# Where the weight sums of the second FFN product are formed, and when its residuals are added

## The chip, the cores and the metric

The kernel runs on one core of a Trainium2 chip. The metric is the time of one execution on the device, in microseconds (us). TensorE (PE in the profile) multiplies matrices, with the loads of its stationary operand shown apart (PEld). VectorE (DVE), ScalarE (ACT) and GpSimd (POOL) do elementwise work. SyncE (SP) issues every transfer between HBM and the on-chip memory (DMA); sixteen DMA engines carry them.

## The reference, cut to what matters

One encoder layer for 17 blocks of 128 tokens: a mixer, a layer norm, a feed-forward network (FFN), and another layer norm. Change and prediction concern the FFN.

```python
D_MODEL = 1024; D_FF = 4 * D_MODEL; ALPHA = 2 ** 0.25
def squared_relu_ffn(x, w1, w2):
    h = jnp.square(jax.nn.relu(jnp.einsum('bld,df->blf', x, w1)))
    return jnp.einsum('blf,fd->bld', h, w2)
...
xp = layer_norm(ALPHA * xp + hp, ln1_g[l], ln1_b[l])                                    # x1 in the kernel
xp = layer_norm(ALPHA * xp + squared_relu_ffn(xp, w_ff1[l], w_ff2[l]), ln2_g[l], ln2_b[l])
```

## The kernel before

The program is one stream: the mixer, the projection `out_proj`, then `ffn`. The order of instructions on each engine is not written by hand. A scheduler takes the program and lets an instruction go out ahead of earlier ones when its operands and its buffer are free by its own timing; the result is a fixed queue for each engine, and an engine works through its queue in order. A buffer of a pool is used again only when its last reader is done, and the transfer that fills it then waits in SP's queue with all that stands behind it.

**Numbers.** Every fp32 operand of the FFN is split into a high and a low part (`split`: a cast on ACT, then a subtraction on DVE), and each product is three matmuls (high·high, high·low, low·high: `PASSES`).

**Seven products for eight.** Both FFN products work on 2x2 blocks and replace eight block products by seven (the scheme of Strassen and Winograd), at the price of sums of blocks on both sides. The products are numbered 1 to 7. `Sums` forms the sums and keeps them in HBM: `x_piece` those of the tokens (`xv`), `w1_piece` those of `w_ff1` (`w1s`), `w2_piece` those of `w_ff2` (`w2s`).

**First product** (matmul line L880). The tokens go in three batches b = 0, 1, 2 (384, 384 and 320 columns, `TOKENS`); in each, 16 steps g over `w_ff1`. A step runs its seven products in the order 1, 6, 2, 7, 5, 4, 3 with 12 matmuls each. A step needs the seven weight blocks of its g (`load_w1`: tiles `w1l`, `w1r`, `w1s`, 1.75 MB), and a batch needs seven token tiles (`load_x`: stage `xr`, two buffers, then `xt`, which are freed by the last step of the batch before). `hc` and `hs` leave as the sums `hv`. In batches 1 and 2 every second step also calls `w2_piece` for one g: it loads the four blocks b11, b12, b21, b22 of `w_ff2` in two transfers of 512 KB (`w2p`), makes T1 = b12 - b11, b22 - b12, T2 = b22 - T1 and T2 - b21 in four subtractions (L792 to L795), and stores them in two transfers of 512 KB (`w2s`). The tiles come from the pool `stage` (tag `st`, three buffers), which `x_piece` uses too (`xts`, `xtt`, `xsum`).

**Second product** (L1068). Seven runs, one for each product i, in the order 1, 2, 6, 7, 5, 3, 4; the last is cut in two. A run has four passes kg over the inner dimension, and a pass three blocks b. A block needs a tile of `hv` (stage `hr`, two buffers, then `ht`, three); a pass needs four weight tiles `w2` of a pool of ten, split from two tiles `w2r` (three buffers). `load_w2` reads `w_ff2` itself for i = 1, 2, 3 and the stored sums `w2s` for 6, 7, 5, 4. The last pass of a run ends each pair of blocks with `evict`, which adds the accumulator to halves of the result tiles `y`. After 5, `evict` also calls `residual` for both tiles of the pair: it loads a whole tile of x1 (512 KB) and adds ALPHA times it to the whole of `y`. After 3 and 4 `finish` does the layer norm. At the end of each run but the last, `odd` does a part of the 17th block (tiles `hor`, L1033).

Of the kernel before, what the change touches and what calls it, by code (L numbers as in the profile page):

```python
# [7 lines left out]
F32 = mybir.dt.float32  # L8
F32R = mybir.dt.float32r
AF = mybir.ActivationFunctionType  # L10
ALU = mybir.AluOpType
# [717 lines left out]
class Sums:  # L729
# [5 lines left out]
    def __init__(self, nc, A, dr, sp, x1_d):  # L735
        self.nc, self.A, self.sp, self.x1_d = nc, A, sp, x1_d
        self.xv = [dr.tile([P, 7, 4, n], F32, name=f"xv{b}") for b, n in enumerate(TOKENS)]
        self.w1 = [dr.tile([P, 2, 1024], F32, name=f"w1s{g}") for g in range(NG)]
        self.w2 = [dr.tile([P, 2, 1024], F32, name=f"w2s{g}") for g in range(NG)]
# [45 lines left out]
    def w2_piece(self, g):  # L785

        nc = self.nc
        w = [self.sp.tile([P, 2, 512], F32, name="w2p", tag="st") for f in range(2)]
        for f in range(2):
            nc.sync.dma_start(w[f].rearrange("p d n -> p (d n)"), self.A["w_ff2"][g][:, f])  # L790
        b11, b12, b21, b22 = (w[f][:, d] for f in range(2) for d in range(2))
        nc.vector.tensor_sub(b11, b12, b11)  # L792
        nc.vector.tensor_sub(b12, b22, b12)
        nc.vector.tensor_sub(b22, b22, b11)
        nc.vector.tensor_sub(b21, b22, b21)  # L795
        for f in range(2):
            nc.sync.dma_start(self.w2[g][:, f], w[f].rearrange("p d n -> p (d n)"))

# [6 lines left out]

    def load_w2(self, to, i, g, n):

        f, d = {1: (0, 0), 2: (1, 0), 3: (1, 1), 5: (0, 0), 7: (0, 1), 4: (1, 0), 6: (1, 1)}[i]
        for k in range(n):
            src = (self.A["w_ff2"] if i < 4 else self.w2)[g + k]  # L810
            self.nc.sync.dma_start(to[:, k], src[:, f, 512 * d:512 * d + 512])
# [3 lines left out]
def ffn(ctx, tc, ps1, A, O, dr, small, sp, rsqrt, split, x1_d, sums):  # L815
# [101 lines left out]
    for k, (b, g) in enumerate(steps):  # L917
        last = k + 1 == len(steps)
        if not last:
            raw = load_w1(*steps[k + 1])  # L920
        X2, W2 = dict(X), {}

        def ahead(i):
            if last:
                return
            W2[i] = split_w1(raw[i])
            if g == NG - 1:
                X2[i] = load_x(b + 1, i)

        ff1(b, g, W, X, ahead)  # L930
        if b < 2 and g in (3, 6, 9):
            sums.x_piece(b + 1, g // 3 - 1)
        if b > 0 and g % 2:
            sums.w2_piece(8 * (b - 1) + g // 2)
        X, W = X2, W2
# [4 lines left out]
    cp = pool("cf", 1, side="right")  # L940
    y = {c: yp.tile([P, D], F32, name=f"y{c}") for c in range(NCH)}
# [20 lines left out]

    def load_w2(i, kg):
        out = []
        for k in range(2):
            s = wr.tile([P, 2, 512], F32, name="w2r", tag="wr")
            sums.load_w2(s, i, 4 * kg + 2 * k, 2)
            out += split_rows(s)
        return out
# [6 lines left out]
    def residual(c, d):  # L976

        x = sp.tile([P, D], F32, name="x1", tag="st")
        nc.sync.dma_start(x, x1_d[c])
        nc.vector.scalar_tensor_tensor(y[c], x, ALPHA, y[c], op0=ALU.mult, op1=ALU.add)  # L980
        stat(c, d)
# [16 lines left out]
    def evict(i, l, r, ps):  # L998
# [9 lines left out]
        if i == 5:  # L1008
            nc.vector.tensor_add(yd, yc, ps)
            nc.vector.tensor_add(yb, yb, ps)  # L1010
            residual(l, 0)
            residual(r, 1)
# [34 lines left out]
    runs = [(i, (0, 1, 2)) for i in (1, 2, 6, 7, 5, 3)] + [(4, (0, 1)), (4, (2,))]  # L1047
# [6 lines left out]
    for k, (i, kg, bs) in enumerate(passes):  # L1054
# [4 lines left out]
        for b in bs:  # L1059
# [3 lines left out]
            for j, (l, r) in enumerate(zip(*THIRDS[b])):  # L1063
                if kg == 0:
                    acc[l] = bank()
                for q, (u, v) in enumerate(PASSES):
                    for m in range(4):
                        nc.tensor.matmul(acc[l], h[:, u, m, j * P:(j + 1) * P], w[m][:, v], start=kg + q + m == 0,  # L1068
                                         stop=(kg, q, m) == (3, 2, 3))
                if kg == 3:  # L1070
                    evict(i, l, r, acc[l])
            h = h2
        w = w2
        if kg == 3 and i != 4:
            n = 2 if i in (5, 3) else 3
# [78 lines left out]
```

## Time and profile before

| | |
|---|---|
| median of 3 runs | 2842.54 us (2840.2 to 2848.67) |
| the profiled execution | 2838.33 us, its span 2836.5 us |
| granted TensorE clock, mean | 0.989 |
| projection `out_proj`, then first product | first product begins at 1478.86 us |
| second product | begins at 2166.78 us; last matmul ends near 2822 us |
| moved by DMA | 708.21 MB, mean 250 GB/s |

The profile gives, for each engine, the busy time and the idle time with what ended it; the timeline lists an engine's instructions in order of time, runs of like ones merged, with the idle time ahead in brackets. The table by stretches gives, for a stretch of the span, each engine's busy time, the granted clock of TensorE (1.00 is full speed), the busy share of the DMA engines and what they moved. Of a transfer the profile shows when SP issued it, and how long it took to land.

### The profile page before, as it was taken

How to read it: one execution, taken by the hardware profiler on the slowest of the kernel's cores; microseconds unless marked ns; L12 is line 12 of the kernel's file. 1: busy time of each engine (PE TensorE's matmuls, PEld its weight loads, DVE VectorE, ACT ScalarE, POOL GpSimd, SP SyncE). 2: the span in 40 equal slices, each digit the busy share in tenths (PEclk: the TensorE clock that was granted, in tenths of full speed). 3: DMA queues.
4: the chain of work that ended last, by engine and by line, in shares of the span. 5: the costliest groups of instructions: out<-in, count | busy, mean ns of one | idle time of the engine just before them, and what ended most of it. 6: DMA issues, size and time to landing. Idle time of an engine off the chain costs nothing.

```text
span 2836.5 us, 42155 instructions
## 1 busy us (share of the span) xinstructions
PE 2755.8 (97%) x15814; PEld 2525.9 (89%) x15814; DVE 1811.7 (64%) x2852; ACT 1097.7 (39%) x2024; POOL 395.0 (14%) x547
## 2 busy tenths in 40 slices
PE   9999999999999998998989998999999999999998
PEld 8988899999999997887869998999999888888886
DVE  6666667645676457665558777767776344544887
ACT  5445423323233332101115555556665333333343
POOL 2224223323234312000100000000000000000022
PEclk9999999999999999999999999999999999999999
DMA  9897898766797769888479999986877455545764
GB/s 316 255 301 247 280 295 258 226 224 212 225 299 228 253 204 306 274 262 264 160 225 356 325 341 354 348 305 241 280 235 237 159 163 187 172 149 180 257 216 167
DMA packets 490012, 708.21 MB, mean 250 GB/s; under 512 B 74304, under 2 KB 378832, under 8 KB 483280
## 3 DMA queue, kind: packets, MB, share of 16 engines
q1 hardware_dynamic: 489808, 705.53, 75.3%
q8 instruction: 124, 2.03, 0.3%
q14 instruction: 80, 0.66, 0.1%
HBM read 474.04 MB, written 231.39 MB: 249 GB/s over the span
## 4 chain that ended last, share of the span: by engine, by line
PE 76%; DMA 12%; DVE 7%; SPq 1%; issue 1%; ACT 1%; POOL 1%; ACTq 0%; DVEq 0%; POOLq 0%
PE pf L880 22%; PE pf L1068 21%; PE psfl L231 12%; PE pstl L239 10%; PE po L683 4%; PE yd L446 2%; DMA w1s<-w1p 2%; DMA w1p<-in_w_ff 2%; PE pf L1033 2%; DMA xv<-xtt 1%; PE sg L537 1%; PE st L483 1%; DMA e<-at 1%; DMA v<-vo 1%; PE yo L489 1%
## 5 line engine op out<-in xcount | busy, mean ns | idle before, releaser
L880 PE MATMUL pf<-xt,w 128*128 128x384 f32 (+1 forms) x4032 | 672.9, 329 | 24.7 <-ACT w L55 13.6
L880 PEld LDWEIGHTS pf<-xt,w 128*128 128x128 f32 x4032 | 669.5, 189 | 28.2 <-ACT w L55 14.4
L1068 PE MATMUL pf<-w,ht 128*128 128x512 f32 x2688 | 618.0, 389 | 0.7 <-ACT ht L55 0.7
L1068 PEld LDWEIGHTS pf<-w,ht 128*128 128x128 f32 x2688 | 504.4, 188 | 105.8 <-ACT ht L55 1.1
L231 PE MATMUL psfl<-xw,w 128*128 128x384 f32 (+1 forms) x2880 | 495.5, 330 | 0.1
L231 PEld LDWEIGHTS psfl<-xw,w 128*128 128x128 f32 x2880 | 475.9, 188 | 9.4 <-issue 9.0
L239 PE MATMUL pstl<-w,xw 128*128 128x256 f32 (+1 forms) x3264 | 410.2, 286 | 8.5 <-ACT w L55 6.6
L239 PEld LDWEIGHTS pstl<-w,xw 128*128 128x128 f32 x3264 | 395.6, 189 | 21.3 <-issue 12.0
L683 PE MATMUL po<-wout,mx 128*128 128x512 f32 x1632 | 378.9, 393 | 14.1 <-ACT mx L55 9.7
L683 PEld LDWEIGHTS po<-wout,mx 128*128 128x128 f32 x1632 | 308.2, 190 | 81.4 <-ACT mx L55 10.7
L56 DVE TENSOR_TENSOR ht<-hr,ht 128x1536 fp32r<-128x1536 f32 (+1 forms) x84 | 132.3, 1576 | 185.2 <-ACT ht L55 183.3
L55 ACT CAST ht<-hr 128x1536 fp32r<-128x1536 f32 (+1 forms) x84 | 112.3, 1337 | 214.8 <-PE pf L1068 192.7
L76 POOL TENSOR_SCALAR frs<-fmv 128x1 f32<-128x1 f32 x17 | 8.9, 525 | 1303.0 <-DVE fmv L987 1302.4
L56 DVE TENSOR_TENSOR w<-w2r,w 128x512 fp32r<-128x512 f32 x192 | 124.5, 684 | 61.1 <-ACT w L55 60.9
L55 ACT CAST w<-w2r 128x512 fp32r<-128x512 f32 x192 | 110.9, 618 | 135.5 <-PE pf L1068 93.4
L55 ACT CAST w<-w1s 128x512 fp32r<-128x512 f32 x192 | 118.1, 619 | 83.7 <-PE pf L880 74.3
L56 DVE TENSOR_TENSOR w<-w1s,w 128x512 fp32r<-128x512 f32 x192 | 131.3, 687 | 25.8 <-ACT w L55 19.9
L308 DVE SCALAR_TENSOR_TENSOR acc<-raw,cw,acc 128x640 f32<-128x640 f32 (+1 forms) x108 | 114.0, 1055 | 18.3 <-ACT acc L302 16.9
L438 ACT ACTIVATE e<-e,nacum 128x128 f32<-128x128 f32 x272 | 83.6, 389 | 71.9 <-POOL e L69 71.9
L247 ACT ACTIVATE gt<-gt 128x256 f32<-128x256 f32 (+1 forms) x116 | 52.3, 451 | 95.2 <-DVE gt L246 95.2
L871 ACT ACTIVATE hc<-hc 128x384 f32<-128x384 f32 (+3 forms) x144 | 87.1, 608 | 2.0
L55 ACT CAST mx<-mxs 128x512 fp32r<-128x512 f32 x34 | 20.1, 620 | 171.2 <-PE po L683 87.2
(214 smaller groups left out, 2856.5 us busy)
## 6 DMA issues: line engine op xcount, KB each, us to landing
w1s<-w1s SPq DMA_DIRECT2D x48, 1024.0 KB, 7.7
hr<-hv SPq DMA_DIRECT2D x56, 768.0 KB, 5.7
w<-w_x SPq DMA_DIRECT2D x12, 2048.0 KB, 10.4
w1r<-in_w_ff SPq DMA_DIRECT2D x48, 512.0 KB, 7.9
hv<-hs SPq DMA_DIRECT2D x32, 768.0 KB, 6.7
w2r<-w2s SPq DMA_DIRECT2D x80, 256.0 KB, 4.6
ws<-in_w_in SPq DMA_DIRECT2D x34, 512.0 KB, 7.5
e<-at SPq DMA_DIRECT2D x34, 512.0 KB, 7.0
```

The costliest lines, as they stand in the source:

```text
L55: nc.scalar.copy(hi, src)
L56: nc.vector.tensor_sub(lo, src, hi.bitcast(F32))
L231: nc.tensor.matmul(ps[:, :n], w[:, a, k, f * P:(f + 1) * P], xw[:, b, k, o:o + n], start=(q, i, k) == KORDER[0], stop=(q, i, k) == KORDER[-1])
L239: nc.tensor.matmul(ps[:, :n], xw[:, a, k, j * P:(j + 1) * P], w[:, b, k, :n], start=(q, i, k) == KORDER[0], stop=(q, i, k) == KORDER[-1])
L308: nc.vector.scalar_tensor_tensor(aa, raw[:, k:k + npr], cw[:, ft, k:k + 1], aa, op0=ALU.mult, op1=ALU.add)
L438: nc.scalar.activation(e[:, h], e[:, h], AF.Exp, bias=s["nacum"][:, i:i + 1])
L446: nc.tensor.matmul(yd[:, h * HD:(h + 1) * HD], e[:, h], xdt[:, h * HD:(h + 1) * HD], start=True, stop=True)
L683: nc.tensor.matmul(acc[c][d], m[c][k // 4][:, a, k % 4], W[q][:, w, i, d * 512:(d + 1) * 512], start=k == 0 and (a, w) == (0, 0), stop=k = ...
L871: nc.scalar.activation(t, t, AF.Square)
L880: nc.tensor.matmul(o, W[i][:, u, k], X[i][:, v, k, :n], start=q + k == 0 and not more, stop=q == 2 and k == 3, skip_group_check=True)
L1033: nc.tensor.matmul(ps[d], h[:, u, k, f], w[d][:, v], start=k + f + q == 0, stop=(k, f, q) == (n - 1, 1, 2))
L1068: nc.tensor.matmul(acc[l], h[:, u, m, j * P:(j + 1) * P], w[m][:, v], start=kg + q + m == 0, stop=(kg, q, m) == (3, 2, 3))
```

## The change

`w2_piece` and the stored `w2s` go. In their place `load_w2` of the second product reads blocks of `w_ff2` and forms the sums itself: for i = 6 it loads b11, b12 and b22, makes T1 and T2 and stores both (`made`, named t0 to t7) beside splitting T2; for i = 7 it loads b12 and b22; for i = 5 it loads T1; for i = 4 it loads b21 and T2. The operands after the first go through a new pool `wt` of three buffers. The last two runs are exchanged (4 ahead of 3). `residual` is done in halves of a tile and in other places: those of half 0 of the left tile in run 6 at kg = 1, the three others in run 4 at kg = 0, 1 and 2.

```diff
-        self.w2 = [dr.tile([P, 2, 1024], F32, name=f"w2s{g}") for g in range(NG)]
...
-    def w2_piece(self, g):
-        nc = self.nc
-        w = [self.sp.tile([P, 2, 512], F32, name="w2p", tag="st") for f in range(2)]
-        for f in range(2):
-            nc.sync.dma_start(w[f].rearrange("p d n -> p (d n)"), self.A["w_ff2"][g][:, f])
-        b11, b12, b21, b22 = (w[f][:, d] for f in range(2) for d in range(2))
-        nc.vector.tensor_sub(b11, b12, b11)
-        nc.vector.tensor_sub(b12, b22, b12)
-        nc.vector.tensor_sub(b22, b22, b11)
-        nc.vector.tensor_sub(b21, b22, b21)
-        for f in range(2):
-            nc.sync.dma_start(self.w2[g][:, f], w[f].rearrange("p d n -> p (d n)"))
...
-        if b > 0 and g % 2:
-            sums.w2_piece(8 * (b - 1) + g // 2)
...
+    wt = pool("wt", 3, side="right")
...
+    made = [dr.tile([2, P, 2, 512], F32, name=f"t{k}") for k in range(2 * KD)]
+    block = lambda f, d: lambda g: [A["w_ff2"][2 * g + m][:, f, 512 * d:512 * d + 512] for m in range(2)]
+    b11, b12, b21, b22 = (block(f, d) for f in range(2) for d in range(2))
+    t1, t2 = (lambda g: [made[g][0]]), (lambda g: [made[g][1]])
+    PARTS = {1: (b11,), 2: (b21,), 3: (b22,), 6: (b11, b12, b22), 7: (b12, b22), 5: (t1,), 4: (b21, t2)}
+
     def load_w2(i, kg):
         out = []
-        for k in range(2):
-            s = wr.tile([P, 2, 512], F32, name="w2r", tag="wr")
-            sums.load_w2(s, i, 4 * kg + 2 * k, 2)
+        for g in (2 * kg, 2 * kg + 1):
+            s = None
+            for n, part in enumerate(PARTS[i]):
+                t = wr.tile([P, 2, 512], F32, name="w2r", tag="wr") if n == 0 else wt.tile([P, 2, 512], F32, name="w2t", tag="wt")
+                src = part(g)
+                if len(src) == 1:
+                    nc.sync.dma_start(t, src[0])
+                else:
+                    for m in range(2):
+                        nc.sync.dma_start(t[:, m], src[m])
+                if n:
+                    nc.vector.tensor_sub(t, t, s)
+                    if i == 6:
+                        nc.sync.dma_start(made[g][n - 1], t)
+                s = t
             out += split_rows(s)
         return out
...
-    def residual(c, d):
-        x = sp.tile([P, D], F32, name="x1", tag="st")
-        nc.sync.dma_start(x, x1_d[c])
-        nc.vector.scalar_tensor_tensor(y[c], x, ALPHA, y[c], op0=ALU.mult, op1=ALU.add)
-        stat(c, d)
+    def residual(c, d, whole):
+        x = sp.tile([P, 512], F32, name="x1", tag="st")
+        h = slice(512 * d, 512 * d + 512)
+        nc.sync.dma_start(x, x1_d[c][:, h])
+        nc.vector.scalar_tensor_tensor(y[c][:, h], x, ALPHA, y[c][:, h], op0=ALU.mult, op1=ALU.add)
+        if whole:
+            stat(c, d)
+
+    def between(i, kg, l, r):
+        if (i, kg) == (6, 1):
+            residual(l, 0, True)
+        if (i, kg) == (4, 0):
+            residual(r, 1, True)
+        if (i, kg) == (4, 1):
+            residual(r, 0, False)
+        if (i, kg) == (4, 2):
+            residual(l, 1, False)
...
-    runs = [(i, (0, 1, 2)) for i in (1, 2, 6, 7, 5, 3)] + [(4, (0, 1)), (4, (2,))]
+    runs = [(i, (0, 1, 2)) for i in (1, 2, 6, 7, 5, 4)] + [(3, (0, 1)), (3, (2,))]
...
+                between(i, kg, l, r)
                 if kg == 3:
                     evict(i, l, r, acc[l])
```

Since the scheduler sets the order, three places show what it made of the change. Each is SP's queue.

The first is the start of the first product; up to its first five rows the two programs are alike. Here x1_15 and x1_16 are the last results of `out_proj` on their way to HBM, the `w1` rows with 14640, 14644, 14642 (before) and 14624, 14628, 14626 (after) are the weights of step g = 2, and `xts` are tokens for the sums of batch 2. Before:

```order
L853 DMA w1s_14507<-w1s1_11521 128x2048
L841 DMA xr_14479<-xv0_11517 128x1536
L769 DMA xv1_11518<-xtt_15930 128x4x128
L851 DMA w1r_14505<-in_w_ff1 128x1024
L790 DMA w2p_17082<-in_w_ff2 128x1024
L790 DMA w2p_17083<-in_w_ff2 128x1024
L841 DMA xr_14487<-xv0_11517 128x1536
L711 DMA x1_15_125<-x1_14374 128x1024
L37 DMA xts_17366<-x1_12_122 32x4x256
L849 DMA w1l_14640<-in_w_ff1 128x4x128
```

Behind the ten rows stand another `xts` of 128 KB, then `w1s_14644` and `w1r_14642`. After:

```order
L831 DMA w1s_14491<-w1s1_11521 128x2048
L819 DMA xr_14463<-xv0_11517 128x1536
L768 DMA xv1_11518<-xtt_15914 128x4x128
L829 DMA w1r_14489<-in_w_ff1 128x1024
L37 DMA xts_17340<-x1_12_122 32x4x256 x4
L819 DMA xr_14471<-xv0_11517 128x1536
L711 DMA x1_15_125<-x1_14358 128x1024
L827 DMA w1l_14624<-in_w_ff1 128x4x128
L831 DMA w1s_14628<-w1s2_11522 128x2048
L829 DMA w1r_14626<-in_w_ff1 128x1024
```

The two `w2p` are gone from ahead of `xr`, 512 KB of tokens stand there instead, and the three weight transfers of g = 2 follow the store of x1_15 with no row between.

The second place is the change from batch 0 to batch 1, where the token tiles `xr` of batch 1 are loaded (16727, 16751, 16773 before and 16711, 16735, 16757 after are those of products 7, 5 and 4). Before:

```order
L841 DMA xr_16727<-xv1_11518 128x1536
L905 DMA hv0_14437<-hc_16642 128x384
L790 DMA w2p_19748<-in_w_ff2 128x1024
L849 DMA w1l_16945<-in_w_ff1 128x4x128
L853 DMA w1s_16949<-w1s2_11522 128x2048
L851 DMA w1r_16947<-in_w_ff1 128x1024
L907 DMA hv0_14437<-hs_16506 128x4x384
L841 DMA xr_16751<-xv1_11518 128x1536
L797 DMA w2s8_11544<-w2p_19462 128x1024
L797 DMA w2s8_11544<-w2p_19463 128x1024
L841 DMA xr_16773<-xv1_11518 128x1536
```

After:

```order
L819 DMA xr_16711<-xv1_11518 128x1536
L883 DMA hv0_14421<-hc_16626 128x384
L827 DMA w1l_16929<-in_w_ff1 128x4x128
L831 DMA w1s_16933<-w1s2_11522 128x2048
L819 DMA xr_16735<-xv1_11518 128x1536
L829 DMA w1r_16931<-in_w_ff1 128x1024
L885 DMA hv0_14421<-hs_16490 128x4x384
L819 DMA xr_16757<-xv1_11518 128x1536
```

One load and two stores of 512 KB are gone from between, as are those ahead of the piece; nothing has come in.

The third place is run 6, where the weights of its second pass (g = 2 and 3, both numbered by pairs as `made` is) are fetched. Before, each is two transfers of 256 KB for a half tile, and nothing else:

```order
L811 DMA w2r_22768<-w2s4_11540 128x512
L811 DMA w2r_22768<-w2s5_11541 128x512
L811 DMA w2r_22777<-w2s6_11542 128x512
L811 DMA w2r_22777<-w2s7_11543 128x512
L811 DMA w2r_22905<-w2s8_11544 128x512
```

After, b11 of pairs 2 to 5 is `w2r_22631`, `22650`, `22788` and `22807`; T1 and T2 of pair 2 are formed in `w2t_22634` and `22639`, whose b12 and b22 were loaded in the run before; T1 of pair 3 in `22653`; b22 of pair 3 goes to `22658`:

```order
L958 DMA w2r_22631<-in_w_ff2 128x512 x2
L958 DMA w2r_22650<-in_w_ff2 128x512 x2
L958 DMA w2r_22788<-in_w_ff2 128x512 x2
L962 DMA t2_21306<-w2t_22634 128x1024
L958 DMA w2r_22807<-in_w_ff2 128x512 x2
L962 DMA t2_21306<-w2t_22639 128x1024
L962 DMA t3_21307<-w2t_22653 128x1024
L958 DMA w2r_22969<-in_w_ff2 128x512
L958 DMA w2t_22658<-in_w_ff2 128x512 x2
```

The load into `w2t_22658` takes the buffer of `w2t_22634`, and so stands behind the store of T1 of pair 2 and waits for its landing; the weights of the second half of the pass come out of `w2t_22658`.

More of the change, by code (lines that the diff above doesn't have):

```diff
@@ L804, in during_out_proj @@
             self.x_piece(0, n // 2 - 2)
[L806 to L811, printed above, removed]
 @with_exitstack
@@ L1010, in evict @@
             nc.vector.tensor_add(yb, yb, ps)
-            residual(l, 0)
-            residual(r, 1)
         if i == 3:
@@ L1073, in ffn @@
         w = w2
-        if kg == 3 and i != 4:
-            n = 2 if i in (5, 3) else 3
+        if kg == 3 and i != 3:
+            n = 2 if i in (5, 4) else 3
             odd(g0, n, g0 == 0, g0 + n == NG)
```

## The prediction

> **What bounds the kernel now.** I read the table of busy times first, then the timeline of TensorE from the start of the first product on, then the table by stretches, then the chain of work that ended last. The busy time (name, us, share of the span):
>
> ```profile
> PE 2755.8 (97%) x15814; PEld 2525.9 (89%) x15814; DVE 1811.7 (64%) x2852; ACT 1097.7 (39%) x2024; POOL 395.0 (14%) x547
> ```
>
> TensorE is busy 97% of the span, and the change neither removes nor adds a matmul. So time can come only from where TensorE waits. Its timeline in the FFN (start, length, and in brackets the wait ahead) has few waits:
>
> ```profile
> 1478.86 4.13 PE L880 MATMUL pf<-xt,w 128*128 128x384 f32 x12 [7.50 <-ACT w L55]
> 1489.13 15.74 PE L880 MATMUL pf<-xt,w 128*128 128x384 f32 x76 [6.15 <-ACT w L55]
> 1505.21 1.65 PE L880 MATMUL pf<-xt,w 128*128 128x384 f32 x8 [0.34 <-DVE xt L56]
> 1509.54 225.32 PE L880 MATMUL pf<-xt,w 128*128 128x384 f32 x1288 [2.67 <-ACT hc L883]
> 1735.13 1.66 PE L880 MATMUL pf<-xt,w 128*128 128x384 f32 x8 [0.28 <-DVE xt L56]
> 1743.89 234.28 PE L880 MATMUL pf<-xt,w 128*128 128x384 f32 x1344 [7.10 <-ACT xt L55]
> 1978.56 188.38 PE L880 MATMUL pf<-xt,w 128*128 128x320 f32 x1284 [0.39 <-ACT xt L55]
> ```
>
> There is a group of waits where the first product starts (7.50, 6.15, 0.34, 2.67), one at the change from batch 0 to 1 (0.28, 7.10), next to none from batch 1 to 2 (0.39). The stretches (length, busy us of PE, PEld, DVE, ACT, POOL with counts, granted clock, DMA share, GB/s):
>
> ```profile
> 1484.00:1510.00 26.00, 17.72 (x85) 16.45 (x86) 23.19 (x32) 13.17 (x21) 2.10 (x4) 0.86 1.04 370
> 1510.00:1720.00 210.00, 210.00 (x1204) 210.00 (x1204) 160.99 (x278) 117.67 (x204) 0.00 (x0) 0.99 0.98 340
> 1720.00:1750.00 30.00, 22.62 (x117) 21.99 (x116) 24.01 (x34) 17.40 (x27) 0.00 (x0) 0.89 1.01 374
> 1960.00:1980.00 20.00, 19.61 (x123) 19.35 (x122) 17.26 (x25) 15.45 (x25) 0.00 (x0) 1.00 0.78 277
> 2365.00:2461.00 96.00, 96.00 (x425) 79.51 (x424) 44.54 (x53) 32.56 (x43) 0.00 (x0) 1.00 0.53 170
> 2822.00:2836.50 14.50, 0.58 (x3) 0.15 (x1) 7.00 (x10) 2.37 (x2) 1.94 (x6) 0.67 0.27 108
> ```
>
> Both places with long waits have full DMA engines (1.04 and 1.01); the batch change with 0.39 us has them at 0.78. In the second product TensorE is busy all the time and DMA half of it, and behind the last matmul a tail of 14.5 us follows.
>
> **The two places that the change relieves.** The chain of work that ended last (start, length) goes through exactly the transfers concerned; two rows of ACT and one of SP complete it:
>
> ```profile
> 1484.43 12.03 DMA w2p<-in_w_ff
> 1496.53 11.37 DMA w1r<-in_w_ff
> ...
> 1730.10 12.25 DMA xr<-xv
> ...
> 1970.38 6.85 DMA xr<-xv
> ```
>
> ```profile
> 1491.03 0.33 SPq L711 DMA_DIRECT2D x<-x  x1
> 1507.97 0.62 ACT L55 CAST w<-w1r 128x512 fp32r<-128x512 f32 x1 [0.84 <-DMA w1r<-in_w_ff]
> 1509.02 0.85 ACT L883 COPY hc<-pf 128x384 f32<-128x384 f32 x2
> 1742.37 1.47 ACT L55 CAST xt<-xr 128x1536 fp32r<-128x1536 f32 x1 [4.76 <-DMA xr<-xv]
> ```
>
> Start: the copies of `hc` stand in ACT's queue behind casts of the weights of g = 2, whose `w1r` was issued at 1496.53, when a `w2p` issued at 1484.43 had landed, and took 11.37 us among 370 GB/s. TensorE waited 2.67 us for the copy. In the new order the three weight transfers stand directly behind the store that went out at 1491.03, so they leave some 3 to 4 us earlier (of the 5.5 between, the issues of two others go off), with 1 MB of `w2p` exchanged for 512 KB of `xts` ahead; 0.5 MB at 370 GB/s is another 1.4 us. That is more than 2.67.
>
> Batch change: the `xr` of product 5 was issued at 1730.10, when its buffer came free, and needed 12.25 us; 1.5 MB of `w2p` and `w2s` stand right beside it in SP's queue (second piece of the order). The like transfer at the next batch change (640 instead of 768 KB) took 6.85. The order of TensorE's matmuls there becomes, product by product, that of the change from batch 1 to 2. With 6.85 x 768/640 = 8.2 us, the cast of 1742.37 comes 4 us earlier; and its predecessor, which waited behind the same traffic, moves too. So the wait shrinks to between 0.39 (its twin) and 7.10 - 4.0 = 3.1. I take 0.8, nearer to the twin, whose order and load it gets.
>
> Each wait also costs what follows it. Short stretches of TensorE (length, busy and count, granted clock, DMA share, GB/s):
>
> ```profile
> 1509.50:1513.50 4.00, 3.96 (x14) 0.57 1.03 380
> 1513.50:1517.50 4.00, 4.00 (x25) 1.00 1.02 421
> 1743.80:1747.80 4.00, 3.90 (x12) 0.50 1.07 411
> 1978.50:1982.50 4.00, 3.94 (x27) 1.00 0.91 264
> ```
>
> An undisturbed stretch of 4 us sees 25 matmuls of 384 columns; after the wait of 2.67 it sees 14, after 7.10 it sees 12. At 225.32/1288 = 0.175 us each, less one or two counted at both edges, that is 1.6 and 2.0 us lost to a clock of about half. After 0.39 us the clock is whole. The Trainium skill (page "TensorE: Matmul & The Clock Gate", section "Part 1: The HAM clock gate") has the clock halved after an idle window of about 3.4 us. By that rule alone the wait of 2.67 us would cost no clock and the sum below would be 1.6 us smaller; the row with 0.57 decides against it here.
>
> Sum of the gains: start 2.67 + 1.6 = 4.3, of which I take 3.8, since the next weights may bind in its place; bounds 0 (they do) and 4.3 + 1.5 (part of the 6.15 also goes, the `w1s` that it waits for having shared the engines with `w2p`). Batch change 0.28 + 7.10 + 2.0 - 0.8 = 8.6; bounds 4.3 (a wait of 3.1 is left, and the clock falls) and 9.0. Together 12.4, from 4.3 to 14.8. The 7.50 at the very start stays, since both programs are alike up to there.
>
> **What the change takes off without gain.** On DVE the subtractions of `w2_piece`, 16 x 4, leave the first product, and 4 x 8 of twice the width come into the second:
>
> ```profile
> L792 DVE TENSOR_TENSOR w2p<-w2p 128x512 f32<-128x512 f32 x16 | 11.0, 685 | 5.9 <-DMA w2p<-in_w_ff 5.6 <-issue 0.3
> L994 DVE TENSOR_TENSOR yo<-yo,g 128x1024 f32<-128x1024 f32 x17 | 20.4, 1208 | 5.8 <-ACT yo L993 5.7
> L980 DVE SCALAR_TENSOR_TENSOR y<-x,y 128x1024 f32<-128x1024 f32 x16 | 19.2, 1211 | 0.0
> ```
>
> 64 x 0.685 = 43.8 us leave, 32 x 1.21 = 38.7 come. Sixteen of them fall in run 6: 19.4 us into a run with 44.5 of 96 us busy; with the eight half residuals moved there (8 x 0.68 for the sum, the same for the statistics: 10.9) DVE is at 75 of 96. The residuals as a whole cost what they did, 32 halves for 16 tiles of 1.21. None of it lies on the path while TensorE has its operands: 0 us. The exchange of the last two runs leaves the tail as it is: the last pair is again evicted, normed and stored by the same row of instructions: 0.
>
> **What it adds: transfers in run 6.** Per run 96 us x 170 GB/s = 16.3 MB before. Run 6 now loads three blocks for one (8.4 MB more) and stores two (8.4 MB): 33.1 MB, 345 GB/s if nothing is ahead. At 0.53 for 170 GB/s the engines would be full at 321; so they come close to full. That alone does not stop TensorE: from 1510 to 1720 it ran 210.00 of 210 us at 340 GB/s. But a chain is new: T1 of a pair is formed, stored, the store lands, its `wt` buffer takes b22 of the next pair, T2 is formed and split. The rows for its links: SP and ACT in run 6, and DMA sizes with the median us to landing, of the second product (first two), of 1750 to 1960 at a DMA share of 0.84 (third) and of 1510 to 1720 (last two).
>
> ```profile
> 2357.09 10.47 SPq L811 DMA_DIRECT2D w2r<-w2s  x10
> ```
>
> ```profile
> 2362.87 2.63 ACT L55 CAST w<-w2r 128x512 fp32r<-128x512 f32 x4 [1.97 <-DMA w2r<-w2s]
> 2380.33 1.67 ACT L55 CAST w<-w2r 128x512 fp32r<-128x512 f32 x3 [3.28 <-PE pf L1068]
> ```
>
> ```profile
> w2r<-w2s SPq DMA_DIRECT2D x48, 256.0 KB, 4.7
> out_y<-yo SPq DMA_DIRECT2D x15, 512.0 KB, 3.2
> w2s<-w2p SPq DMA_DIRECT2D x14, 512.0 KB, 6.1
> w2p<-in_w_ff SPq DMA_DIRECT2D x15, 512.0 KB, 8.9
> w2s<-w2p SPq DMA_DIRECT2D x14, 512.0 KB, 9.6
> ```
>
> The weights of the second pass are requested from 2357.09 on, and TensorE leaves the first pass at 2380.33: a budget of 23.2 us. Chain: b11 lands (2362.87 - 2357.09 = 5.8), T1 1.2, its store s, b22 l, T2 1.2, two casts 1.2. With s = 3.2 and l = 4.7 that is 17.3, 5.9 early. With 9.6 and 8.9 it is 27.9, 4.7 late, and up to 2 more behind residuals on DVE. I take s = 6.1, l = 6.5 (between 4.7 and 8.9, for engines fuller than before but not full) and the 2 us: 24.0, 0.8 late, where the clock holds. After that three buffers go round: l + s + 3.2 (DVE's two links and a wait) per three tiles, two tiles a pair, 10.5 us per pair against TensorE's 96/8 = 12. So later pairs keep up. Cost of run 6: 1.5 us, bounds 0 and 25 (third rival). Behind a late load SP holds the `hr` of coming blocks, but two `hr` and three `ht` are ahead.
>
> **The sum.** -12.4 + 1.5 = -10.9 against the profiled execution's 2838.33, that is 2827.4; the median of the runs shown lies 4.2 us above that execution, so I give 2842.5 - 10.9 = 2831.6 for the median. About 0.3% (8.5 us) is what a measurement of this kernel can tell from no change.
>
> **Rivals.** First, the batch change stays slow: its wait comes from `xr` going through two buffers one after another (load, cast, split, next load), not from the traffic. For it: the issue at 1730.10 waited for a buffer. Against it: the twin with the same chain waits 0.39. Then the gain is 4.3 there and 2 at the start, less 1.5: 2837.7, no change that can be told. Second, the chain of run 6 runs at middle landings: at s and l of 8, 4 us late once with 2 of clock, and near TensorE's pace after: 7 instead of 1.5, 2837. The third ends slower, by the same chain with the engines full: 6.7 us late at the second pass, then 8.9 + 9.6 + 3.2 = 21.7 per three tiles, 14.5 per pair, 2.5 behind for each of five pairs (12.5), and the clock lost at three passes (6): 25. That gives 2842.5 - 12.4 + 25 = 2855. It decides from a run 6 that loses over 12.4 + 8.5 = 21 us, with landings like those of 1510 to 1720. For it speak 345 GB/s against 321; against it that pairs 0 and 1 are done and three `wt` loads out before the run begins. The Trainium skill (page "DMA: Bandwidth & Descriptors", section "Where 436 GB/s comes from") names about 358 GB/s as the HBM limit of a core. By it run 6 would just fit, and cost nothing; the stretches with 370 and 374 agree that 321 is no hard limit.
>
> **Chances.** The forecast 0.56 (its own range 2826 to 2834); the first rival 0.17; the second 0.17; the third 0.10. Faster by over 0.3% (below 2834): the forecast and a little of the next two, 0.58. Within 0.3%: 0.32. Slower: 0.10. The range runs from the best case, 2842.5 - 14.8 = 2827.7, less 2 for the spread of medians, to 2848, which leaves out most of the third rival.
>
> **What would show it.** Right: no wait near 1507; a wait under 1.5 us where batch 1 begins, an `xr` landing of 7 to 9 us there, and a clock of 1.00 after it; DMA share of 1510 to 1720 near 0.75; in run 6 a DMA share near 0.95 and at most one wait of TensorE, at its second pass, under 3 us. Wrong: a wait over 3 us at the batch change with light traffic (first rival), or TensorE waiting for casts of `w2t` at several passes of run 6 (third).

## The result, and the profile after

The changed kernel took 2826.54 us (median of 5 runs, 2822.72 to 2829.38), the kernel before in the same comparison 2842.54 (5 runs, 2836.27 to 2848.67); the ratio is 0.9939, 95% interval 0.9918 to 0.9961. Two more comparisons of the same two programs (below) gave 0.9955 and 0.9962. Weighted by their intervals the three give 0.9953 [0.9942, 0.9964]: 13 us less, between 10 and 16. The forecast was 10.9 less.

The profiled execution of the changed kernel took 2822.72 us, its span 2821.0. Its table of busy times (name, us, share, count) differs little:

```profile
PE 2753.9 (98%) x15814; PEld 2525.6 (90%) x15814; DVE 1816.1 (64%) x2836; ACT 1096.0 (39%) x2024; POOL 395.1 (14%) x547
```

TensorE is 1.9 us less busy and 13.6 us less idle. The timeline of TensorE in the first product (start, length, in brackets the wait ahead) shows where:

```profile
1474.66 4.71 PE L858 MATMUL pf<-xt,w 128*128 128x384 f32 x12 [6.76 <-ACT w L55]
1483.99 17.69 PE L858 MATMUL pf<-xt,w 128*128 128x384 f32 x84 [4.62 <-ACT w L55]
1503.87 226.69 PE L858 MATMUL pf<-xt,w 128*128 128x384 f32 x1296 [2.19 <-ACT hc L861]
1731.02 232.24 PE L858 MATMUL pf<-xt,w 128*128 128x384 f32 x1344 [0.47 <-ACT xt L55]
1963.67 186.54 PE L858 MATMUL pf<-xt,w 128*128 128x320 f32 x1269 [0.42 <-ACT xt L55]
```

The 7.10 us at the change from batch 0 to 1 became 0.47. The 2.67 us for `hc` at the start are still 2.19. In the second product the profile lists no wait of TensorE any more, run 6 included. The table by stretches (length, busy us of PE, PEld, DVE, ACT, POOL, granted clock, DMA share, GB/s), with run 6 in the last row:

```profile
1484.00:1510.00 26.00, 23.81 (x111) 23.40 (x112) 23.88 (x33) 14.71 (x24) 0.02 (x1) 0.82 1.06 355
1510.00:1720.00 210.00, 210.00 (x1212) 210.00 (x1212) 145.61 (x248) 119.67 (x209) 0.00 (x0) 1.00 0.77 263
1720.00:1750.00 30.00, 29.53 (x170) 29.21 (x169) 25.57 (x38) 20.58 (x33) 0.00 (x0) 1.00 0.96 351
1731.00:1735.00 4.00, 3.98 (x23) 3.98 (x24) 4.00 (x6) 4.00 (x8) 0.00 (x0) 1.00 0.84 257
2347.00:2442.00 95.00, 95.00 (x421) 78.68 (x420) 58.57 (x64) 31.67 (x41) 0.00 (x0) 1.00 0.91 315
```

Batch 0 now runs at a DMA share of 0.77 instead of 0.98, and the clock behind the batch change is whole. Run 6 carries 315 GB/s at 0.91, a little less than the prediction worked out (345, near 0.95). The chain of work that ended last still goes through the start and the batch change (start, length):

```profile
1480.06 10.91 DMA xts<-x
1491.03 11.19 DMA w1r<-in_w_ff
1722.23 7.24 DMA xr<-xv
```

`xr` at the batch change needs 7.24 us instead of 12.25; `w1r` at the start needs 11.19, as before (11.37).

**Where the time came from.** In the stages of the FFN, each time from the timeline of TensorE, with a second profile of either program beside the first (the two programs once more, below), in us:

| stage | before | after | gain |
|---|---|---|---|
| begin of the projection's last matmul to first matmul of the FFN | 7.9, 8.9 | 7.2, 7.5 | 1.1 |
| from there to the end of the wait for `hc` | 30.7, 30.5 | 29.2, 29.7 | 1.1 |
| from there to the end of the wait where batch 1 begins | 234.4, 234.7 | 227.2, 227.5 | 7.2 |
| from there to the end of the wait where batch 2 begins | 234.7, 234.2 | 232.7, 232.7 | 1.8 |
| from there to the end of the span | 857.9, 858.0 | 857.3, 857.1 | 0.8 |

These are 12.0 us. With a third profile of the changed kernel (under the last heading of the experiments) the mean gain is 12.6. Ahead of the first row the two programs are alike, but their times are not: the last matmul of the projection began at 1471.0 us before and 1467.5 after, and those 3.5 us of the difference of these two profiles are no effect of the change.

### The profile page after: what moved, and what is told of

It is laid out like the page before. It is cut to its first block, busy times and chain, and to the rows that moved or that the text cites. A ratio compares the mean times of both kernels' runs of the same rounds, so it can differ in the third digit from the quotient of the medians.

```text
span 2821.0 us, 42133 instructions
## 1 busy us (share of the span) xinstructions
PE 2753.9 (98%) x15814; PEld 2525.6 (90%) x15814; DVE 1816.1 (64%) x2836; ACT 1096.0 (39%) x2024; POOL 395.1 (14%) x547
## 4 chain that ended last, share of the span: by engine, by line
PE 77%; DMA 12%; DVE 6%; issue 1%; ACT 1%; POOL 1%; SPq 1%; DVEq 0%; ACTq 0%; POOLq 0%
PE pf L858 22%; PE pf L1075 22%; PE psfl L231 13%; PE pstl L239 10%; PE po L683 4%; PE yd L446 2%; DMA w1p<-in_w_ff 2%; DMA w1s<-w1p 2%; PE pf L1040 2%; DMA v<-v 1%; DMA xv<-xtt 1%; PE st L483 1%; DMA v<-vo 1%; DMA e<-at 1%; PE yo L489 1%
## 5 line engine op out<-in xcount | busy, mean ns | idle before, releaser
L56 DVE TENSOR_TENSOR w<-w2r,w 128x512 fp32r<-128x512 f32 x144 | 93.8, 686 | 36.8 <-ACT w L55 36.6
L55 ACT CAST w<-w2r 128x512 fp32r<-128x512 f32 x144 | 83.3, 618 | 87.3 <-PE pf L1075 56.9
L55 ACT CAST w<-w1r 128x512 fp32r<-128x512 f32 x96 | 59.4, 618 | 98.6 <-PE pf L858 95.3
```

The lines of the kernel that those rows point to most:

```text
L55: nc.scalar.copy(hi, src)
L56: nc.vector.tensor_sub(lo, src, hi.bitcast(F32))
```

## The experiments

The stage that the change works on is read best from a fixed place, so for each run I give two spans beside the ratio: from the first matmul of the first product to the end ("FFN"), and from the begin of the projection's last matmul to the end ("from the projection"). Before they are 1357.6 and 1365.5, after 1346.3 and 1353.5.

### The two programs once more

```diff
(none: the kernel before, and the kernel after)
```

> The kernel before once more, unchanged. Theory (the change works in the FFN alone, about -11 us from the first matmul of the first product to the end, and the rest of the measured -16 us is scatter of what runs ahead of it): ratio 0.997 to 1.003 against itself; first matmul of the first product anywhere between 1474 and 1480 us, the FFN from there 1357.6 +- 1.5 us long again. Rival (kernels that keep the stored sums of w_ff2 are slower ahead of the FFN as well): the first matmul comes at 1478 to 1480 us again.

> The changed kernel once more. Theory: ratio 0.994 to 0.997; from the first matmul of the first product to the end 1346.3 +- 1.5 us; first matmul anywhere between 1474 and 1480 us. Rival (systematic gain ahead of the FFN): ratio near 0.994, first matmul at 1474 to 1475 us again.

Measured: the kernel before against itself 0.9986 [0.9972, 1.0000], 12 runs against 26; FFN 1357.4, from the projection 1366.4. The changed kernel 0.9955 [0.9936, 0.9974], median 2827.64; FFN 1347.0, from the projection 1354.5. The first matmul of the FFN came at 1476.6 and 1477.4 us, not where the rivals had it. So the two spans of one program repeat within 1 us here (a third profile of the changed kernel, below, is 2.5 to 3.1 us shorter than this one), while the whole time of the same program came out 4 us different between two groups of runs. A median of 3 or 5 runs of this kernel is uncertain by some us: its 26 single runs lie between 2833.74 and 2852.27.

### Without the piece, without moving it anywhere

```diff
-        if b > 0 and g % 2:
-            sums.w2_piece(8 * (b - 1) + g // 2)
...
-            src = (self.A["w_ff2"] if i < 4 else self.w2)[g + k]
+            src = self.A["w_ff2"][g + k]
```

> The kernel before with the forming and storing of the sums of w_ff2 left out of the first product; the second product reads blocks of w_ff2 in their place, same sizes and number of loads, so its result is not the FFN's. Residuals and order of runs as before. Theory (all of the gain comes from the transfers that leave the first product): the FFN 11 +- 1.5 us shorter than before, wait at the change from batch 0 to 1 under 1 us with full clock after it; ratio 0.994 to 0.997. Rival (the residuals in halves bring a part): clearly less than 11 us.

Measured: 0.9956 [0.9940, 0.9972], median 2829.17; FFN 1345.9, from the projection 1353.4. At the batch change:

```profile
1743.26 232.25 PE L880 MATMUL pf<-xt,w 128*128 128x384 f32 x1344 [0.38 <-ACT xt L55]
1976.19 24.06 PE L880 MATMUL pf<-xt,w 128*128 128x320 f32 x160 [0.67 <-ACT xt L55]
```

Taking the piece away brings all the gain, and forming the sums in the second product costs nothing that shows beside it. This profile's span is 2834.5 us, only 2 less than before: the last matmul of its projection began 10 us later (1481.1). Read by the span alone, the kernel would have seemed to gain nothing.

### The residuals and the exchange of runs alone, in the kernel before

```diff
-            residual(l, 0)
-            residual(r, 1)
...
-    runs = [(i, (0, 1, 2)) for i in (1, 2, 6, 7, 5, 3)] + [(4, (0, 1)), (4, (2,))]
+    runs = [(i, (0, 1, 2)) for i in (1, 2, 6, 7, 5, 4)] + [(3, (0, 1)), (3, (2,))]
...
+                between(i, kg, l, r)
```

> The kernel before with only the residuals in halves and the last two runs exchanged; the sums of w_ff2 stay in the first product. Theory: nothing, FFN 1357.6 +- 1.5 us, ratio 0.997 to 1.003, the wait of 7 us at the batch change stays. Rival (the residuals bring a part): FFN 2 us or more shorter.

Measured: 0.9991 [0.9974, 1.0008], median 2839.35; FFN 1354.1, from the projection 1361.9. By the number that is the rival's case (2 us or more), but of the 3.5 us in the FFN only 0.9 lie behind batch 2's begin (857.1 against 857.9, where a wait of 0.7 for `ht` went). The rest lies where this edit does nothing: 1.0 at the start, 1.6 at the batch change, whose wait was 5.44 here and 7.10 and 6.21 in the two profiles of before. So the residuals bring about 0.9 us, and a profile of one execution is uncertain by 1 to 2 us at a place that waits for DMA.

### The piece's transfers, or its subtractions

```diff
 # transfers alone
-        nc.vector.tensor_sub(b11, b12, b11)
-        nc.vector.tensor_sub(b12, b22, b12)
-        nc.vector.tensor_sub(b22, b22, b11)
-        nc.vector.tensor_sub(b21, b22, b21)
 # subtractions alone
-            nc.sync.dma_start(w[f].rearrange("p d n -> p (d n)"), self.A["w_ff2"][g][:, f])
+            nc.gpsimd.memset(w[f], 1.0)
...
-        for f in range(2):
-            nc.sync.dma_start(self.w2[g][:, f], w[f].rearrange("p d n -> p (d n)"))
```

(The second also reads `w_ff2` in place of `w2s`, as the run without the piece.)

> The kernel before with the four subtractions of w2_piece left out: its loads and stores stay, so what is stored are the blocks and not their sums, and the FFN's result is another. Theory (the traffic of w2_piece cost the time): from the first matmul of the first product to the end 1357.5 +- 2 us as before, a wait of 5 to 7 us at the change from batch 0 to 1. Rival (the four subtractions held up DVE's queue): near 1346 us, that wait under 1.5 us.

> The kernel before with the loads and stores of w2_piece left out and its four subtractions kept, on tiles that GpSimd fills with a constant; the second product reads blocks of w_ff2 in place of the sums, so the FFN's result is another. Theory (traffic): 1346 to 1348 us from the first matmul of the first product to the end, wait at the batch change under 1.5 us with full clock after it. Rival (DVE): 1353 us or more.

Measured: transfers alone 1.0013 [0.9999, 1.0026], FFN 1358.1; subtractions alone 0.9961 [0.9948, 0.9975], FFN 1345.7. The timeline of TensorE at the batch change with the transfers alone, and then the stretch ahead of it:

```profile
1728.26 3.08 PE L876 MATMUL pf<-xt,w 128*128 128x384 f32 x16 [1.26 <-ACT hc L879]
1732.30 1.66 PE L876 MATMUL pf<-xt,w 128*128 128x384 f32 x8 [0.97 <-DVE xt L56]
1739.26 234.49 PE L876 MATMUL pf<-xt,w 128*128 128x384 f32 x1344 [5.30 <-ACT xt L55]
```

```profile
1510.00:1720.00 210.00, 210.00 (x1212) 210.00 (x1211) 148.34 (x249) 119.50 (x208) 0.00 (x0) 1.00 0.99 344
```

The same with the subtractions alone:

```profile
1727.38 232.23 PE L878 MATMUL pf<-xt,w 128*128 128x384 f32 x1344 [1.35 <-ACT xt L55]
```

```profile
1510.00:1720.00 210.00, 210.00 (x1212) 210.00 (x1211) 179.67 (x314) 118.07 (x205) 28.54 (x30) 1.00 0.80 273
```

With DVE lightly loaded (148 of 210 us) and DMA full the waits stay, 7.5 us together; with DVE more loaded than in the kernel before (180 of 210 against 161) and DMA at 0.80 all but 1.35 us goes. The piece cost its time by its traffic and not by its arithmetic. Since the two buffers of `xr` are the same in both, this also ends the first rival, by which their chain and not the traffic made the wait.

### Two buffers for the operands that T1 and T2 are formed from

```diff
-    wt = pool("wt", 3, side="right")
+    wt = pool("wt", 2, side="right")
```

> The changed kernel with two buffers in the new pool wt instead of three. The theory says that run 6 is held by the round of load, subtraction and store through these buffers: with landings of 6.4 and 5.9 us as in the changed kernel a pair then takes about 6.4 + 3.2 + 5.9 = 15.5 us against some 11 of TensorE, so TensorE waits at the passes of run 6, 10 to 25 us in all, with a lower clock after each wait; ratio 0.999 to 1.005 against the kernel before. Rival (run 6 has much room): under 2 us, ratio as the changed kernel.

Measured: 0.9970 [0.9953, 0.9987], FFN 1352.5, that is 6.2 us more than the changed kernel's profile. The timeline of TensorE in run 6, and the first 4 us behind either wait:

```profile
2397.29 21.69 PE L1075 MATMUL pf<-w,ht 128*128 128x512 f32 x94 [0.83 <-ACT w L55]
2421.11 22.11 PE L1075 MATMUL pf<-w,ht 128*128 128x512 f32 x89 [2.12 <-ACT w L55]
```

```profile
2397.20:2401.20 4.00, 3.91 (x17) 3.07 (x18) 3.40 (x4) 1.52 (x3) 0.00 (x0) 1.00 0.89 216
2421.00:2425.00 4.00, 3.89 (x11) 3.07 (x12) 3.41 (x4) 1.53 (x3) 0.00 (x0) 0.63 0.95 246
```

Run 6 lasts 100.9 us from its first matmul to that of run 7, against 95.7: 2.9 us of waits for casts of `w2t` in front of two passes, and the clock behind the second. That is far less than the 10 to 25 us of waits expected. The landings were shorter than taken, 5.4 us in the median (loads into `w2t`) and 4.4 (stores of T1 and T2) instead of 6.4 and 5.9; by them, and the same 3.2, a pair takes 13.0 us and not 15.5. Still, the chain that the prediction set up for run 6 is real and binds with one buffer less, at the price of 5.3 us; the kernel's third buffer takes it off the path.

### The sums moved, the residuals as before

```diff
             nc.vector.tensor_add(yb, yb, ps)
+            residual(l, 0)
+            residual(r, 1)
...
-    runs = [(i, (0, 1, 2)) for i in (1, 2, 6, 7, 5, 4)] + [(3, (0, 1)), (3, (2,))]
+    runs = [(i, (0, 1, 2)) for i in (1, 2, 6, 7, 5, 3)] + [(4, (0, 1)), (4, (2,))]
...
-                between(i, kg, l, r)
```

> The changed kernel with the residuals as before (whole tiles after the fifth product, runs 3 and 4 in the old order); only the sums are formed in the second product. Theory: 1346 to 1348 us from the first matmul of the first product to the end, ratio as the changed kernel within 0.2%. Rival (the residuals in halves are needed, else DVE or the transfers of the x1 tiles hold up the last runs): 1350 us or more, with waits of TensorE in the last three runs.

Measured: 0.9989 [0.9977, 1.0001], median 2835.03; FFN 1352.3, 6 us more than the changed kernel. Its first product is as fast (677.3 us to the second product, against 677.6). The loss is in the last two runs, as the rival had it. TensorE, then DVE, then ACT, at the last pass:

```profile
2815.90 2.76 PE L1064 MATMUL pf<-w,ht 128*128 128x512 f32 x10 [2.45 <-ACT w L55]
2819.01 3.76 PE L1064 MATMUL pf<-w,ht 128*128 128x512 f32 x14 [0.35 <-DVE w L56]
```

```profile
2810.53 1.22 DVE L960 TENSOR_TENSOR w2t<-w2t,w2r 128x1024 f32<-128x1024 f32 x1
...
2812.80 1.22 DVE L960 TENSOR_TENSOR w2t<-w2t,w2r 128x1024 f32<-128x1024 f32 x1
```

```profile
2814.10 1.24 ACT L989 ACTIVATE yo<-y,fnm,frs 128x1024 f32<-128x1024 f32 x1 [6.22 <-POOL fnm L987]
2815.24 2.17 ACT L55 CAST w<-w2t 128x512 fp32r<-128x512 f32 x4
```

Product 4 now needs a subtraction (b21 and T2) for its weights. With 4 as the last run these subtractions stand on DVE, and the casts on ACT, among the layer norm of finished blocks, and the last pass waits 2.8 us for them. The last run takes 95.6 us against 91.7 in the changed kernel, and the tail behind the last matmul 15.3 against 13.9: 5.3 us together. The run ahead takes 1.0 longer, 0.7 of it a wait for `ht`, and so it does in the kernel before, whose residuals stand where they do here. In the kernel before, the last run and the tail, with product 4 last too and the residuals in the same places, take 91.7 and 13.9. So the 5.3 us come from the moved sums with 4 last, and not from the residuals. With 3 last, whose weights are plain blocks of `w_ff2`, none of this stands there: the exchange, costed at nothing, keeps the moved sums off the end.

### The tokens' sums held back

```diff
-    def tokens(self, c):
+    def tokens(self, c, late=None):
         s = self.sp.tile([P, 4, 256], F32, name="xts", tag="st")
+        if late is not None:
+            self.nc.gpsimd.tensor_copy(s[:, 0, :1], late)
...
-        ff1(b, g, W, X, ahead)
+        late = ff1(b, g, W, X, ahead)
         if b < 2 and g in (3, 6, 9):
-            sums.x_piece(b + 1, g // 3 - 1)
+            sums.x_piece(b + 1, g // 3 - 1, late)
```

(`late` is one column of `hc` of the step; the first of these runs gives it only where b is 1, the second always.)

> The changed kernel, with the sums of batch 2's tokens held back: their tiles are first touched by GpSimd with a value of hc of the step in which the program has them (batch 1, g = 3, 6, 9), so that no load of them can run ahead into the start of the first product. What stands around them stays. Theory (the start's remaining wait of 2.19 us for the copy of hc comes from the w1r of g = 2, which landed in 11.19 us beside 1 MB of token loads, DMA share 1.06): w1r lands in 7 to 9 us, the wait falls to 0 to 0.7, and the FFN, from its first matmul to the end of the span, goes from 1346.6 to 1343 to 1345. Rival (the engines are full there by the weights and token tiles of batch 0 alone, or SP sends the w1r no earlier): the wait stays at 1.5 to 2.7, the FFN at 1346 to 1347.5. The other waits of the start (6.76, 4.62) stay by both. In the timing 0.994 to 0.996 of the kernel before by either, too close to tell apart by it alone.

> As the run before, with the sums of batch 1's tokens held back too (to batch 0, g = 3, 6, 9), which in the changed kernel run ahead into the projection: 8 loads and 7 stores of each of three pieces, the last of them between 1455 and 1480 us, in SP's queue ahead of the first weights. Theory (the same: the start is bound by landings and by SP's queue): the waits of 6.76 and 4.62 us at the first product lose 4 to 8 us together besides the 2.19, so that the time from 0.992 to 0.9945 of the kernel before, 2820 to 2827 us, beats both kernels by 4 to 10 us. Rival (the first product's start waits for the last result of the projection and its casts, not for transfers): the waits of 6.76 and 4.62 stay within 1 us, ratio 0.995 to 0.997. A third way: the held back sums make batch 0 as full as w2_piece made batch 1 and 2, and the wait at the batch change comes back (over 2 us); against it: 8 MB in 235 us, 35 GB/s on 263.

> The changed kernel once more, beside the two others on the same chip. Theory (the change is worth 11 us, all of it in the FFN, and the rest of the first ratio, 0.9939, is what runs ahead of the first product, which is alike in both programs and whose end lay between 1472.4 and 1488.6 us in ten profiles): ratio 0.9945 to 0.9975 with 0.996 in the middle, FFN 1346 to 1347 in the profile, whatever the span. Rival (the change also makes the part ahead of the first product 3 to 5 us faster): ratio 0.9925 to 0.9945.

Measured, in the same order: 0.9951 [0.9934, 0.9968], 0.9936 [0.9914, 0.9958], 0.9962 [0.9944, 0.9980]. FFN 1344.0, 1346.1, 1343.9; from the projection 1351.5, 1346.3, 1352.0. The changed kernel's third profile is thus shorter than the 1346 to 1347 expected; 1.6 us of that lie behind the wait for `hc` (227.2 and 227.5 us to the batch change in the first two profiles, 225.6 in this one). The start of the first with its DMA sizes and landings from 1478 to 1510 (KB, median us):

```profile
1507.16 18.16 PE L860 MATMUL pf<-xt,w 128*128 128x384 f32 x103 [1.09 <-ACT hc L863]
```

```profile
w1r<-in_w_ff SPq DMA_DIRECT2D x3, 512.0 KB, 8.9
```

Without batch 2's tokens at the start the `w1r` land in 8.9 us, the one of g = 2 in 8.0 instead of 11.2, and the wait for `hc` is 1.09 instead of 2.19, a little more than the theory's 0 to 0.7. From the first matmul to the end of this wait are 27.2 us instead of 28.7 to 29.7. A new wait of 1.09 us stands at 1799.58, and in the whole time the gain is too little to see. With both batches held back:

```profile
1479.81 1.58 PE L860 MATMUL pf<-xt,w 128*128 128x384 f32 x8
1482.46 0.96 PE L860 MATMUL pf<-xt,w 128*128 128x384 f32 x4 [1.07 <-DVE w L56]
1484.58 14.90 PE L860 MATMUL pf<-xt,w 128*128 128x384 f32 x76 [1.16 <-ACT w L55]
1501.40 1.66 PE L860 MATMUL pf<-xt,w 128*128 128x384 f32 x8 [1.92 <-DVE xt L56]
1506.96 58.93 PE L860 MATMUL pf<-xt,w 128*128 128x384 f32 x329 [3.89 <-ACT hc L863]
```

The first product begins right behind the projection: its wait (6.76, 7.14 and 7.69 in the three profiles of the changed kernel) is gone, and the next (4.62) is 1.16. The wait for `hc` grew to 3.89, behind a `w1r` and an `xr` that land late. The wait at the batch change is 0.27, so the third way did not come about. Net from the projection: 6 to 8 us less than the changed kernel's 1352.0 to 1354.5. The first ratio did not yet tell the version from the changed kernel, so it was timed again:

> The version with both batches' token sums held back, timed once more, because its first ratio, 0.9936 [0.9914, 0.9958], does not yet tell it from the changed kernel's three (0.9939, 0.9955, 0.9962). Theory (it saves what its profile shows: the 7 to 8 us between the projection's last matmul and the first product go, of which 2 to 3 come back as longer waits for hc and xt behind it): 0.992 to 0.9945, and from the projection's last matmul to the end of the span about 1347, against 1352.3 to 1354.4 of the changed kernel. Rival (the first result was scatter of what runs ahead of the projection's end): ratio 0.995 to 0.997 with the same 1347 in the profile or with 1352.

Measured: 0.9911 [0.9889, 0.9933], median 2818.61; from the projection 1346.0. Together its two ratios are 0.9924 [0.9908, 0.9939], below the changed kernel's 0.9953 [0.9942, 0.9964]. This version beats both kernels, by about 22 and 8 us.

## Why the prediction was right or wrong

**The mechanism held; the step that failed is the range's lower end.** The first ratio, applied to 2842.54, gives 2825.2 us, 0.5 below the lower end of 2825.7. "Less 2 for the spread of medians" was too little: the first ratio's interval alone is 6 us to either side, and the same program against itself came out 4 us apart. The saving did not exceed the best case: 12.6 us by stages and 13 by all three ratios (2829.2 us, inside the range), against 14.8. The medians 2826.54, 2827.64 and 2831.44 lie in the range too, the last on the forecast of 2831.6. That the sum came out near is in part luck: it took the start 2 to 3 us too high, and made up for it by 1.5 us for run 6 that were not lost and 0.9 us from the residuals that it left out.

- **Start of the first product, 3.8 taken, 1.1 measured** (1.4 with the third profile). The 1.1 of the table's first row belong to a wait that the prediction left as it was, and two profiles of the kernel before differ by 1.0 there. The step "that is more than 2.67" failed. The weights do stand right behind the store, and followed it by 3.2 us instead of 5.5, but the store itself went out 13.1 us behind the first matmul instead of 12.2. SP, at the start of the changed kernel:

```profile
1480.06 4.60 SPq L37 DMA_DIRECT2D xts<-x  x4
1487.79 0.34 SPq L711 DMA_DIRECT2D x<-x  x1
1491.03 0.33 SPq L829 DMA_DIRECT2D w1r<-in_w_ff  x1
```

 What the prediction passed over is in its own rows. In both traces, from 1440 us on, no transfer goes out before the eighth ahead of it on SP's queue has landed (their landings are told by eight semaphores, used in turn). Before, the eighth ahead of this `w1r` is the `w2p` that landed at 1484.43 + 12.03 = 1496.46, and `w1r` went out at 1496.53. After, it is the first of four `xts`: it landed at 1480.06 + 10.91 = 1490.97, and `w1r` went out at 1491.03. Among the eight stood two `w2p` and two `xts`, and now stand four `xts`: fewer bytes, but as many transfers, and a small one holds its place until it lands as a large one does. So `w1r` left only 1.3 us earlier, counted from the first matmul, and landed as slowly among as full engines (1.06):

```profile
1502.30 0.62 ACT L55 CAST w<-w1r 128x512 fp32r<-128x512 f32 x1 [1.14 <-DMA w1r<-in_w_ff]
1502.83 0.61 ACT L55 CAST w<-w1s 128x512 fp32r<-128x512 f32 x1
1503.35 0.85 ACT L861 COPY hc<-pf 128x384 f32<-128x384 f32 x2
```

 The copy of `hc` still stands behind two casts of the weights of g = 2. That the tokens held these weights up, the run with batch 2's sums held back shows. With batch 1's held back too, the wait is 3.89 all the same: the first product then begins some 7 us sooner, and `w1r` lands in 10.0 us without any tokens beside it. The term was inside its bounds (0 to 5.8), near the lower one that the prediction named: the next weights bind.
- **Batch change, 8.6 taken, 9.0 measured** (7.2 and 1.8; 9.6 with the third profile, of which some 0.5 come from its whole clock behind `hc`). Right in cause (the runs with the piece's transfers or its subtractions alone: the traffic), in the landing (8.2 estimated, 7.24), in the wait left (0.8 taken, 0.47), and in the clock behind it (whole). The price of the clock, 1.6 to 2.0, is the 1.8 of the table's fourth row.
- **Run 6, 1.5 taken off, nothing measured.** The landings were as taken: s 6.1 estimated, 5.9; l 6.5 estimated, 6.4 (KB and median us, run 6 of the changed kernel):

```profile
w2t<-in_w_ff SPq DMA_DIRECT2D x28, 256.0 KB, 6.4
t<-w2t SPq DMA_DIRECT2D x12, 512.0 KB, 5.9
```

 The chain ended in time, but only just. The casts of T2 for the second and third pass, where by their first matmuls the passes began at 2366.28 and 2388.04:

```profile
2365.19 1.14 ACT L55 CAST w<-w2t 128x512 fp32r<-128x512 f32 x2 [8.47 <-DVE w2t L960]
...
2387.22 1.14 ACT L55 CAST w<-w2t 128x512 fp32r<-128x512 f32 x2 [5.74 <-DVE w2t L960]
```

 The last of these casts ended 0.1 and 0.3 us behind those starts, when the first half of the pass's weights was already in use. With nothing lost to residuals on DVE, for which 2 us were set down, the prediction's 24.0 us are 22.0, inside its budget of 23.2. This rules out the second and third rivals here; the run with two buffers shows how near they were.
- **Residuals and exchange, 0 taken.** The residuals gave 0.9 (the wait for `ht` of 0.7 and a little behind it). The exchange was not idle: with product 4 last, the end costs 5.3 us more (the run with the sums moved alone). The net was nearly right and its reasoning wrong, since it priced the exchange against the old kernel's last run and not against a last run whose weights need DVE.
- **The lower end.** It allowed 2 us for the spread of medians. Single runs of one program spread over 20 us (25 of the kernel before, timed beside the third profile: 2831.9 to 2853.59), and the same program against itself gave 0.9986, that is 4 us. With 4 in place of 2 the range would have begun at 2823.7.

Of what the prediction said would show it right: the batch change, its landing, its clock, the share of 0.77 and run 6's 0.91 came as told; the wait near 1507 did not go. And the longest wait, the 7.50 us that the prediction left standing, could be had: the version with the token sums held back takes it away.

## What to carry to other kernels

A piece of work that nobody waits for still costs what its transfers do to those that somebody waits for: look at the DMA share ahead of each wait, and move bytes to a stage with room (0.53 here) rather than save arithmetic. Count the transfers as well as the bytes: where a queue lets out a transfer only when the eighth ahead of it has landed, a small one holds its place as a large one does. A moved sum takes its operand chain along, so ask of every later place (here the last run, beside the layer norm) whether that chain may end there. Where single runs scatter by more than the effect, compare stages from a fixed instruction on, in two or more profiles of either program, and give the median's own spread its place in the range.

## What the runs showed of the hardware

**A wait of 2 to 2.7 us may or may not cost the clock.** The prediction took from one row that 2.67 us does. Eleven such waits now stand: a granted clock of 0.57 to 0.69 in the 4 us behind 2.12, 2.19, 2.31, 2.67 (twice) and 2.70 us, and of 1.00 behind 2.00, 2.09, 2.43, 2.45 and 2.52. Four of them, each with the stretch of 4 us behind it, of the changed kernel (2.19), its second (2.31) and third profile (2.09), and the version timed twice (2.52):

```profile
1503.50:1507.50 4.00, 3.63 (x12) 3.63 (x13) 3.69 (x7) 0.70 (x2) 0.00 (x0) 0.57 1.08 339
```

```profile
1507.00:1511.00 4.00, 3.93 (x15) 3.93 (x16) 3.95 (x8) 1.09 (x4) 0.00 (x0) 0.66 1.10 340
```

```profile
1511.90:1515.90 4.00, 3.94 (x23) 3.94 (x24) 3.54 (x7) 1.94 (x6) 0.00 (x0) 1.00 1.08 346
```

```profile
1505.00:1509.00 4.00, 3.86 (x22) 3.86 (x23) 3.96 (x8) 0.53 (x3) 0.00 (x0) 1.00 0.55 227
```

The waits of 3.3 to 7.1 us that were looked at (3.28, 3.66, 3.89, 5.30, 5.44, 6.21, 7.10) had 0.50 to 0.65 behind them, those of 0.47, 0.83 and 1.35 had 1.00. Two shorter waits close behind another were followed by a low clock too: with batch 1's token sums held back, waits of 1.16 and 1.64 us, each begun 1.0 us behind the end of a wait of 1.07, had 0.61 and 0.50 behind them (the 4 us from 1484.5 and from 1484.6). So a price for the clock behind a wait near 2.3 us is a chance of about a half, and that alone moves one execution by 1.6 us: the third profile's stretch from `hc` to the batch change is 225.6 us against 227.2 and 227.5. The Trainium skill (page "TensorE: Matmul & The Clock Gate", section "Part 1: The HAM clock gate") names an idle window of about 3.4 us and calls it free-running, so that the number of slow matmuls varies from run to run. That the outcome varies agrees; that a wait must be longer than 3.4 us does not, by the six low clocks behind 2.12 to 2.70 us. What decides between the two outcomes no run here shows.

**The part ahead of the FFN scatters with the same program.** The last matmul of the projection began between 1466.1 and 1481.1 us in twelve profiles of programs that are alike up to there (those with batch 1's tokens held back are left out). What sets it was not tried.
